# A trunk of matmuls whose 512-column streams are turned round

## The chip, the core and the metric

The kernel runs on one core of one Trainium2 chip. A core has a matmul engine (TensorE; PE in the profile, its weight loads PEld), three engines for elementwise work (VectorE or DVE, ScalarE or ACT, GpSimd or POOL), and a queue that issues DMAs (SyncE or SP). Matmuls read SBUF and write PSUM, which has banks of 512 float32 columns on 128 partitions. The metric is the device time of one execution in microseconds (us), given as the median of the runs.

## The reference

Two groups of 512 tokens (a prompt and a sample), 1024 wide, pass through the same two layers: differential attention with 8 heads, then a bidirectional retention with 8 heads. Both layers project, mix, normalise by head, gate and project back.

```python
def trunk(x, ...):
    for i in range(DEPTH):                        # DEPTH = 2
        h = rms_norm(x, norm_g[i], NORM_EPS)
        if i % N_MIXERS == 0:
            x = x + diff_attention(h, da_w_in[j], ...)
        else:
            x = x + bidir_retention(h, ret_w_in[j], ...)
    return rms_norm(x, final_norm_g, NORM_EPS)

def diff_attention(h, ...):
    q, k, v, gate = jnp.split(h @ w_in, ...)      # w_in: 1024 x 8192
    s = jnp.einsum('bqhd,bkhd->bhqk', rotary_half(q), rotary_half(k))
    p = softmax(s);  a = p[:, :, 0] - lam * p[:, :, 1]
    o = jnp.einsum('bhqk,bkhe->bqhe', a, v)
    return (rms_norm(o, subln_g, SUBLN_EPS) * silu(gate)) @ w_out   # w_out: 2048 x 1024

def bidir_retention(h, ...):
    q, k, v, gate = jnp.split(h @ w_in, ...)      # w_in: 1024 x 6144
    o = retention_direction(q, k, v, ...) + flip(retention_direction(flip(q), flip(k), flip(v), ...))
    return (rms_norm(o, subln_g, SUBLN_EPS) * silu(gate)) @ w_out
```

## The kernel before

Each float32 operand is split into two parts of a rounded float32 type (`hi_of`, L400, on ScalarE, and `lo_of`, L403, on VectorE), and each product is three matmuls, hi by hi, hi by lo and lo by hi (`PASSES`), added up in one PSUM bank.

**Projections.** The normalised activations of both token groups stand transposed in SBUF as the operands of a seven-product scheme (`Bop`, products P1 to P7). A `Unit` covers 256 columns of an input weight; of its two kinds, "pair" (queries, keys, gates) has weights stationary and streams 512 tokens, and "wide" (values) has activations stationary and streams 256 weight columns. `product` issues them: `pair` at L599, 12 matmuls of 512 columns for a product (4 slices of the contraction by 3 passes), `wide` at L609, 48 of 256 columns. Banks come from the rings `pj` (3), `sc` (2), `o` (2) and `tp` (1).

**Attention.** For each head, group and tile of 128 queries: `scores` (L1116) makes two score banks with 3 matmuls of 512 columns each, `row_max` (L1124) and `exps` (L1134) the softmax, `combine` the difference, `transp` (L1161) four transposes, and for every second tile `av` (L1181) 24 matmuls of 256 columns.

**Output projections.** `out_step` (L891) makes one block of 128 tokens by 512 columns of one head's contribution with 6 matmuls, and VectorE (L896) adds it to the residual. The last block of the second layer is done in two halves of 256 columns.

**Retention.** Its products (L1315, L1339, L1359, L1367) stream 256 columns.

Eight matmuls of 512 columns at L1010, on plain float32 zeros, run ahead of all work while the inputs arrive.

A planner (`Plan`) takes all operations with assumed costs, places them on the five engines in a simulated schedule, and writes out that order; what a matmul costs in it is a constant in the program (0.7 us for the three matmuls of `scores`, 2.79 for the twelve of `pair`, 1.39 for the six of `out_step`).

Of the kernel before, what the change touches and what calls it, by code (L numbers as in the profile page):

```python
# [15 lines left out]
P = 128  # L16
# [237 lines left out]
def trunk_kernel(  # L254
# [7 lines left out]
    nc = tc.nc  # L262
# [90 lines left out]
    def bank(tag, name=None):  # L353
        return Buf(plan, tag, BUFS[tag], lambda i: view(pj if tag == "pj" else sc, tag, i, S, [P, S]))
# [19 lines left out]
    def axpy(n, fn, r, w):  # L374

        plan.op("DVE", 0.13 + 0.00104 * n, fn, r, w)
# [13 lines left out]
    def pe(cost, fn, r, w, wait=0.0):  # L390
        plan.op("PE", cost, fn, r, w, wait=wait)
# [126 lines left out]
    class Unit:  # L518
# [67 lines left out]
        def product(self, op):  # L586
            which = BANK_OF[op]
            n_banks = 2 if self.wide else 1
            opens = op in OPENS
            if opens:  # L590
                self.banks[which] = [bank(self.tags[which], which) for _ in range(n_banks)]
            a, b = self.ops.pop(op), B_OF[op]
            bt = [Bop[b, k] for k in range(4)]
            reads = [q[1] for q in a] + bt

            def pair(ps, ks=range(4)):
                for k in ks:
                    for i, (u, v) in enumerate(PASSES):
                        nc.tensor.matmul(  # L599
                            ps.t, a[u][0]()[:, k, :], bt[k][:, v, :], start=(opens and k == 0 and i == 0),  # L600
                            stop=(k == 3 and i == 2), skip_group_check=True)

            def wide(ps, t):
                if self.led and op == "P1" and t == 0:
                    for j in range(NT):
                        nc.tensor.transpose(ps[:, j * P:(j + 1) * P], ident.t, ident.t)
                for k in range(4):
                    for i, (u, v) in enumerate(PASSES):
                        nc.tensor.matmul(  # L609
                            ps[:, (t % 2) * 256:(t % 2) * 256 + 256], bt[k][:, v, t * P:(t + 1) * P],  # L610
                            a[u][0]()[:, k, :], start=(opens and t % 2 == 0 and k == 0 and i == 0),
                            stop=(k == 3 and i == 2), skip_group_check=True)

            if not self.wide:
                ps = self.banks[which][0]
                if op == "P1" and self in first_units[:2]:
                    for k in range(4):
                        pe(0.7, lambda k=k: pair(ps, (k,)), reads[:2] + [bt[k]], [(ps, k)])
                else:
                    pe(2.79, lambda: pair(ps), reads, [ps])  # L620
                return
            for t in range(NT):
                ps = self.banks[which][t // 2]
                led = self.led and op == "P1" and t == 0
                pe(1.87 if led else 1.43, lambda ps=ps, t=t: wide(ps, t), reads + [ident] * led, [ps])
# [236 lines left out]
    def out_weights(w, h, i):  # L862
        r = raw_t([P, 2, S])
        src = w[h * 256:(h + 1) * 256, i * S:(i + 1) * S].rearrange("(e p) c -> p e c", p=P)
        dma(lambda: r.t, lambda: src, [], [r], 512)
        hi, lo = ws_t([P, 2, S]), ws_t([P, 2, S])
        hi_of(1024, lambda: hi.t, lambda: r.t, [r], [hi])
        lo_of(1024, lambda: lo.t, lambda: r.t, lambda: hi.t, [r, hi], [lo])
        wsn[h, i] = (hi, lo)

    def out_step(w, h, g, t, i, o, rr, last, parts=1):


        owed[h, g] -= 1
        if (h, i) not in wsn:
            out_weights(w, h, i)
        banks = [bank("pj") for _ in range(parts)]
        u = wsn[h, i]
        x = xN[g, t]
        n = S // parts  # L880
        for p in range(parts):
            here = slice(p * n, (p + 1) * n)
            part = (x, i) if parts == 1 else (x, (i, p))

            ps = banks[p]

            def fn(here=here, ps=ps):
                m = 0
                for e in range(2):
                    for a, b in PASSES:  # L890
                        nc.tensor.matmul(ps[:, here], o[a][:, e, t * P:(t + 1) * P], u[b][:, e, here],  # L891
                                         start=(m == 0), stop=(m == 5))
                        m += 1
            pe(1.39 / parts, fn, [(o[0], t // 2), (o[1], t // 2), *u], [ps])
            half = x[:, i * S + p * n:i * S + (p + 1) * n]
            axpy(n, lambda half=half, here=here, ps=ps: nc.vector.scalar_tensor_tensor(  # L896
                half, ps[:, here], rr[:, t % 2:t % 2 + 1], half, op0=ALU.mult, op1=ALU.add),
                [ps, part, rr], [part])
            if h == NH - 1:
                last(g, t, i, half, n, part, i == 1 and p == parts - 1)  # L900
# [206 lines left out]
    def scores(i):  # L1107
        h, g, t = tiles[i]
        st[i]['s'] = []
        for j in range(2):  # L1110
            s = bank("sc")
            q, k = qk[h, g, j, 0], qk[h, g, j, 1]

            def fn(s=s, q=q, k=k):
                for n, (a, b) in enumerate(PASSES):
                    nc.tensor.matmul(s.t, q[:, a, t * P:(t + 1) * P], k[:, b, :], start=(n == 0), stop=(n == 2))  # L1116
            pe(0.7, fn, [q, k], [s])
            st[i]['s'].append(s)

# [333 lines left out]
    for i in range(N2 + 1):  # L1453
        if i < N2:
            b, c = chunks[i]
# [78 lines left out]
```

## Time and profile before

| | |
|---|---|
| median of 3 runs | 1808.89 us (1808.3 to 1814.46) |
| span of the profiled execution | 1807.0 us |
| TensorE busy | 1794.9 us, 99% of the span |
| weight loads (PEld) | 1558.1 us, 86% |
| VectorE busy | 1477.1 us, 82% |
| ScalarE busy | 895.1 us, 50% |
| GpSimd busy | 169.5 us, 9% |
| DMA queue with the most traffic | 326.71 MB, 54.1% of 16 engines |

The span runs from the first to the last instruction of the profiled execution; that execution has no time of its own beside the span, and the median of the timed runs lies 1.9 us above it. A matmul's record in the profile is longer than the distance to the next matmul's start, because matmuls overlap in the engine and their ends are modelled; lengths of back-to-back pieces give the distance.

### The profile page before, as it was taken

The page shows a single profiled execution, that of the slowest core. Times are in us where ns is not written, and L with a number is a line of the kernel's source. Part 1 is how long each engine was busy: PE and PEld are TensorE (multiplying, and loading weights), DVE is VectorE, ACT ScalarE, POOL GpSimd, SP SyncE. Part 2 cuts the span into 40 slices and gives each one's busy share as a digit, 9 for nine tenths or more (in the row PEclk, how much of TensorE's full clock was granted, in tenths as well). Part 3 has the DMA queues.
Part 4 walks back from the last instruction along what each step waited for, and adds up shares of the span by engine and source line. Part 5 has one row for each costly group of instructions (what it writes and reads, how often), then busy time and mean ns, then how long its engine had stood idle before and what let it go on. Part 6 is the DMA issues. An engine that isn't in the chain of part 4 may idle for free.

```text
span 1807.0 us, 27780 instructions
## 1 busy us (share of the span) xinstructions
PE 1794.9 (99%) x10299; PEld 1558.1 (86%) x10299; DVE 1477.1 (82%) x2319; ACT 895.1 (50%) x1856; POOL 169.5 (9%) x323
## 2 busy tenths in 40 slices
PE   9999999999999999999999999999999999999998
PEld 6789889898988888888888888898989898888887
DVE  7958787778699888888888897787887967888887
ACT  7753444433434565554555866444434355444346
POOL 1000000000000022222322300000000000111113
PEclk9999999999999999999999999999999999999999
DMA  6444455555545685444554524464657559765662
GB/s 217 134 126 137 161 140 178 184 168 155 174 126 175 201 334 198 178 156 159 190 204 140 190 73 146 140 210 146 205 156 228 151 170 396 272 238 182 225 218 94
DMA packets 162767, 328.81 MB, mean 182 GB/s; under 512 B 12724, under 2 KB 76872, under 8 KB 162632
## 3 DMA queue, kind: packets, MB, share of 16 engines
q1 hardware_dynamic: 162304, 326.71, 54.1%
q8 instruction: 81, 1.33, 0.3%
q14 instruction: 54, 0.44, 0.1%
q10 hardware_dynamic: 328, 0.34, 0.1%
HBM read 209.55 MB, written 117.44 MB: 181 GB/s over the span
## 4 chain that ended last, share of the span: by engine, by line
PE 93%; DVE 2%; DMA 2%; ACT 2%; issue 1%; POOL 0%; SPq 0%; POOLq 0%; DVEq 0%; ACTq 0%
PE pj L599 20%; PE pj L891 19%; PE sc L599 10%; PE pj L609 10%; PE o L599 8%; PE o L1181 5%; PE sc L1116 5%; PE sc L609 5%; PE o L609 2%; PE o L1359 2%; PE tp L1161 2%; PE sc L1315 1%; PE o L1367 1%; PE tp L1339 1%; DMA raw<-in_ret_w_out_dram 1%
## 5 line engine op out<-in xcount | busy, mean ns | idle before, releaser
L891 PE MATMUL pj<-ws,arena 128*128 128x512 f32 x1542 | 391.2, 397 | 0.0
L891 PEld LDWEIGHTS pj<-ws,arena 128*128 128x128 f32 x1542 | 277.7, 188 | 52.7
L599 PE MATMUL pj<-b,ws 128*128 128x512 f32 x1080 | 265.0, 392 | 0.0
L599 PEld LDWEIGHTS pj<-b,ws 128*128 128x128 f32 x1080 | 201.4, 188 | 43.0
L403 DVE TENSOR_TENSOR ws<-st,ws 128x512 fp32r<-128x512 f32 (+1 forms) x192 | 147.9, 774 | 74.8 <-ACT ws L400 56.7
L896 DVE SCALAR_TENSOR_TENSOR b<-pj,crr,b 128x512 f32<-128x512 f32 (+1 forms) x257 | 189.9, 744 | 21.4 <-PE pj L891 21.0
L403 DVE TENSOR_TENSOR ws<-raw,ws 128x512 fp32r<-128x512 f32 (+1 forms) x164 | 141.5, 868 | 71.3 <-ACT ws L400 61.0
L400 ACT CAST ws<-st 128x512 fp32r<-128x512 f32 (+1 forms) x192 | 132.4, 693 | 121.4 <-PE pj L599 36.4
L599 PE MATMUL sc<-arena,ws 128*128 128x512 f32 x768 | 186.8, 392 | 0.0
L599 PE MATMUL o<-arena,ws 128*128 128x512 f32 x744 | 180.0, 393 | 1.1 <-ACT m L385 0.6
L599 PEld LDWEIGHTS sc<-arena,ws 128*128 128x128 f32 x768 | 144.0, 188 | 31.3
L400 ACT CAST ws<-raw 128x512 fp32r<-128x512 f32 (+1 forms) x164 | 125.7, 772 | 87.0 <-PE o L599 45.0
L599 PEld LDWEIGHTS o<-arena,ws 128*128 128x128 f32 x744 | 138.4, 188 | 31.7 <-DVE arena L463 1.4
L599 PE MATMUL pj<-arena,ws 128*128 128x512 f32 x648 | 160.3, 392 | 0.4 <-DVE arena L463 0.4
L599 PEld LDWEIGHTS pj<-arena,ws 128*128 128x128 f32 x648 | 120.8, 188 | 26.7 <-DVE arena L463 0.7
L1134 ACT ACTIVATE b<-sc,nm 128x512 f32<-128x512 f32 x128 | 88.0, 689 | 66.9 <-DVE nm L1124 66.5
L636 ACT COPY c<-pj 128x512 f32<-128x512 f32 x104 | 60.9, 586 | 119.7 <-PE pj L599 66.4
L609 PE MATMUL pj<-ws,b 128*128 128x256 f32 x960 | 116.8, 276 | 0.0
L609 PEld LDWEIGHTS pj<-ws,b 128*128 128x128 f32 x960 | 113.2, 188 | 0.7
L1116 PE MATMUL sc<-arena 128*128 128x512 f32 x384 | 101.2, 395 | 0.3 <-ACT b L1134 0.3
L1181 PEld LDWEIGHTS o<-arena 128*128 128x128 f32 x768 | 93.1, 188 | 2.7
L1181 PE MATMUL o<-arena 128*128 128x256 f32 x768 | 93.7, 278 | 0.0
(207 smaller groups left out, 2855.9 us busy)
## 6 DMA issues: line engine op xcount, KB each, us to landing
qk<-os SPq DMA_DIRECT2D x192, 256.0 KB, 3.6
arena<-qk SPq DMA_DIRECT2D x96, 512.0 KB, 5.8
raw<-in_da_w_in_dram SPq DMA_DIRECT2D x64, 512.0 KB, 5.1
v<-os SPq DMA_DIRECT2D x64, 512.0 KB, 4.3
arena<-v SPq DMA_DIRECT2D x64, 512.0 KB, 4.1
raw<-in_ret_w_in_dram SPq DMA_DIRECT2D x48, 512.0 KB, 4.8
os<-g SPq DMA_DIRECT2D x32, 512.0 KB, 7.4
g<-e SPq DMA_DIRECT2D x48, 256.0 KB, 4.6
```

Of the source, the lines that this page charges most:

```text
L400: act(n, lambda: nc.scalar.copy(dst(), src()), r, w)
L403: dve(n, lambda: nc.vector.tensor_tensor(dst(), src(), hi().bitcast(F32), op=ALU.subtract), r, w)
L599: nc.tensor.matmul(ps.t, a[u][0]()[:, k, :], bt[k][:, v, :], start=(opens and k == 0 and i == 0), stop=(k == 3 and i == 2), skip_group_che ...
L609: nc.tensor.matmul(ps[:, (t % 2) * 256:(t % 2) * 256 + 256], bt[k][:, v, t * P:(t + 1) * P], a[u][0]()[:, k, :], start=(opens and t % 2 == ...
L636: act(S, lambda c=c, ps=ps: nc.scalar.copy(c.t, ps.t), [ps], [c])
L891: nc.tensor.matmul(ps[:, here], o[a][:, e, t * P:(t + 1) * P], u[b][:, e, here], start=(m == 0), stop=(m == 5))
L896: axpy(n, lambda half=half, here=here, ps=ps: nc.vector.scalar_tensor_tensor(half, ps[:, here], rr[:, t % 2:t % 2 + 1], half, op0=ALU.mult ...
L1116: nc.tensor.matmul(s.t, q[:, a, t * P:(t + 1) * P], k[:, b, :], start=(n == 0), stop=(n == 2))
L1134: act(840, lambda j=j, s=s, m=m: nc.scalar.activation(p[:, j, :], s.t, AF.Exp, bias=m.t, accum_out=sm[:, 2 * j + n:2 * j + n + 1]), [s, m] ...
L1161: nc.tensor.transpose(tp[:, j * P:(j + 1) * P], p[:, 0, j * P:(j + 1) * P], ident.t)
L1181: nc.tensor.matmul(o[:, e * 256:(e + 1) * 256], v[b][:, j, e * P:(e + 1) * P], aT[a][:, j, :], start=(n == 0), stop=(n % 12 == 11), skip_g ...
L1359: nc.tensor.matmul(o[:, e * 256:(e + 1) * 256], v_[v][:, 2 * c + j, e * P:(e + 1) * P], a_[:, u, j * 256:(j + 1) * 256], start=(e == 0 and ...
```

## The change

In three places a matmul's moving operand and its PSUM output are indexed from the last column to the first, with a step of -1. Every column's sum lands where it did before, and within a bank all matmuls of a sum go in the same direction. The stationary operand is indexed as before.

```diff
@@ pair, in Unit.product @@
                         nc.tensor.matmul(
-                            ps.t, a[u][0]()[:, k, :], bt[k][:, v, :], start=(opens and k == 0 and i == 0),
+                            ps[:, ::-1], a[u][0]()[:, k, :], bt[k][:, v, ::-1], start=(opens and k == 0 and i == 0),
                             stop=(k == 3 and i == 2), skip_group_check=True)
@@ out_step @@
-                        nc.tensor.matmul(ps[:, here], o[a][:, e, t * P:(t + 1) * P], u[b][:, e, here],
+                        nc.tensor.matmul(ps[:, here][:, ::-1], o[a][:, e, t * P:(t + 1) * P], u[b][:, e, here][:, ::-1],
                                          start=(m == 0), stop=(m == 5))
@@ scores @@
-                    nc.tensor.matmul(s.t, q[:, a, t * P:(t + 1) * P], k[:, b, :], start=(n == 0), stop=(n == 2))
+                    nc.tensor.matmul(s[:, ::-1], q[:, a, t * P:(t + 1) * P], k[:, b, ::-1],
+                                     start=(n == 0), stop=(n == 2))
```

The last block of the second layer's output projection, in two halves of 256 columns, is indexed by the second of these places too.

## The prediction

> **What bounds the kernel now.** I read the page first: busy times, then the granted clock, then the chain of waits.
>
> ```profile
> span 1807.0 us, 27780 instructions
> PE 1794.9 (99%) x10299; PEld 1558.1 (86%) x10299; DVE 1477.1 (82%) x2319; ACT 895.1 (50%) x1856; POOL 169.5 (9%) x323
> PEclk9999999999999999999999999999999999999999
> PE 93%; DVE 2%; DMA 2%; ACT 2%; issue 1%; POOL 0%; SPq 0%; POOLq 0%; DVEq 0%; ACTq 0%
> ```
>
> TensorE has work in flight for 1794.9 of 1807.0 us, so it idles for only 12.1 us; it holds 93% of the chain that ended last, and its clock is granted at 90% or more in every slice. The next engine, DVE, is 330 us short of the span. The profiled execution spans 1807.0 us; the three timed runs have a median of 1808.89, so I add 1.9 us for what lies around the span. Then I asked what TensorE waited for (the view of waits, TensorE alone: us in total, times, longest).
>
> ```profile
> PE sc L1010 <- DVE minus L411: 1.4, 1, 1.4
> PE tp L1028 <- DVE arena L463: 1.0, 2, 0.7
> PE o L1028 <- DVE b L387: 0.6, 1, 0.6
> PE o L599 <- ACT m L385: 0.6, 1, 0.6
> ```
>
> These are the four longest lines; all waits together are under 5 us. There is next to no slack in which a longer matmul could hide and no stall that a shorter one would expose early: what one matmul gains or loses, the span gains or loses. So the question is the pace of one 512-column matmul, and the number of them. The instruction groups of TensorE, shapes kept apart (busy us, mean ns of one record):
>
> ```profile
> L891 PE MATMUL pj<-ws,arena 128*128 128x512 f32 x1530 | 389.8, 398 | 0.0
> L599 PE MATMUL pj<-b,ws 128*128 128x512 f32 x1080 | 265.0, 392 | 0.0
> L599 PE MATMUL sc<-arena,ws 128*128 128x512 f32 x768 | 186.8, 392 | 0.0
> L599 PE MATMUL o<-arena,ws 128*128 128x512 f32 x744 | 180.0, 393 | 1.1 <-ACT m L385 0.6 <-DVE arena L463 0.3
> L599 PE MATMUL pj<-arena,ws 128*128 128x512 f32 x648 | 160.3, 392 | 0.4 <-DVE arena L463 0.4
> L599 PE MATMUL sc<-b,ws 128*128 128x512 f32 x120 | 29.1, 391 | 0.0
> L1116 PE MATMUL sc<-arena 128*128 128x512 f32 x384 | 101.2, 395 | 0.3 <-ACT b L1134 0.3
> L609 PE MATMUL pj<-ws,b 128*128 128x256 f32 x960 | 116.8, 276 | 0.0
> L1161 PE MATMUL tp<-ident,b 128*128 128x128 f32 x256 | 38.4, 272 | 0.0
> ```
>
> L599 has 1080 + 768 + 744 + 648 + 120 = 3360 matmuls of 512 columns, L891 1530, L1116 384: 5274 that the change turns round. A record is longer than the pace, since matmuls overlap; the pace comes from the pieces of the chain (start us, length us, what), where nothing lies between instructions:
>
> ```profile
> 75.27 8.24 PE pj L599 x36
> 163.58 5.47 PE o L609 x48
> 705.89 1.39 PE pj L891 x6
> 707.28 2.83 PE o L1181 x24
> 710.11 1.40 PE sc L1116 x6
> 711.51 0.44 PE tp L1161 x4
> 713.35 1.38 PE sc L1116 x6
> 719.53 2.74 PE o L1181 x24
> ```
>
> Paces: L599 8.24/36 = 228.9 ns; L891 1.39/6 = 231.7; L1116 1.39/6 (mean of two pieces) = 231.7; 256 columns at L609 5.47/48 = 114.0; 128 columns at L1161 0.44/4 = 110. A record is thus its pace plus a tail that doesn't depend on the width: 392 - 228.9 = 163 at 512 columns, 276 - 114 = 162 at 256, 272 - 110 = 162 at 128. The 5274 take 3360 x 0.2289 + 1914 x 0.2317 = 769 + 443 = 1213 us, two thirds of the span.
>
> **The change, part by part.** No instruction is added, removed or moved: built from both kernels, the order on all five engines is the same, DMA issues included, and so is each count. What changes in a matmul is two patterns: the moving operand's (start at the last column, step -1 for 1) and the bank's. The weights' pattern stays. The eight warm-up matmuls, the 256-column ones (L609, L1181, L1315 and the rest) and the transposes stay as they are; only the split last block of L891, 12 matmuls of 256 columns, turns too, worth 12 x 0.1 = 1 us at half rate and left out of the sum.
>
> The semaphore waits change in 24 places, all on DVE. Five subtractions that write a weight split lose a wait for TensorE; DVE isn't the bound, so that is worth nothing. Nineteen of the row maxima over the scores gain a wait for ACT. What it protects is a column of the four-deep ring that the exponential two tiles earlier read; the scores' own matmul has already waited for a later exponential to free its bank, so I cost this at nothing. If that cover were gone, DVE would stand for one exponential each time:
>
> ```profile
> L1134 ACT ACTIVATE b<-sc,nm x128: 672/690/704, 628.1 to 1004.4; 128x512 f32<-128x512 f32 x128
> L1010 PE MATMUL sc<-e x16: 592/592/1220, 1.4 to 10.9; 128*128 128x512 f32 x16
> 1.44 10.09 PE L1010 MATMUL sc<-e 128*128 128x512 f32 x16 [1.44 <-DVE minus L411]
> ```
>
> 19 x 0.69 = 13 us of DVE, behind which are queued the combinations of the probabilities and the evacuations of the output banks; TensorE runs other blocks meanwhile, so under 13 us at the worst.
>
> What is left is the price of a descending column stream. No row shows one: every matmul of this trace reads and writes ascending, contiguous columns. The nearest rows give the bounds. The trace has two column rates at a granted clock of 90% or more. The fast one is 512 columns in 229 ns and 256 in 114: 2.2 columns per ns. The slow one is the last two rows above: L1010 streams the same 512 columns, and its record is 592 at the minimum and the median, so its pace is 592 - 163 = 429 ns, 1.2 columns per ns; the transposes of L1161, in the middle of the run, have 128 columns in 110 ns, 1.2 too. Those rows read plain float32 where the fast ones read the rounded kind, so the slow rate has its own reason there; what it shows is the step in which this engine falls back: to half. The fast rate takes two columns where the slow one takes one. [...]
>
> Bounds of the unknown price, per matmul: from below, the best column rate that any row shows, 2 x 114.0 = 228 ns, no loss and a gain of 1 to 4 ns; from above, L1010's first rows: if nine of its sixteen run at 429 (the median equals the minimum), the other seven take (10.09 - 0.16 - 9 x 0.429)/7 = 867 ns each, a quarter of the fast rate. Between these I take 429, the row of the same width, at the median of that group; and as the upper end of this case twice the best pace, 456 ns, where the small excess of the fast rate is doubled as well.
>
> The Trainium skill, page "SBUF — State Buffer", section "Door 1: The DMA port swizzle", speaks to both sides: reads within one 16-byte line run at full bandwidth from two hits in the line on, while a PSUM line holds two float32 values and any non-contiguous PSUM pattern slows matmuls significantly. Its first half would make the descending read free and the time that of before; its second half speaks against this change if a step of -1 counts as non-contiguous, and gives no figure. No row here shows either.
>
> The sum: L599 3360 x (429 - 228.9) = 672 us; L891 1530 x (429 - 231.7) = 302; L1116 384 x (429 - 231.7) = 76; together 1050 us. Nothing is taken off for waits that vanish (under 5 us). 1807 + 1050 + 1.9 = **2859 us**. With 456 ns for 429, 5274 x 0.027 = 142 us more: 3001. If all 12.1 us of TensorE's idle time were used up on the way, it would be 2847. So the case's own range is 2845 to 3000. DVE, ACT and DMA do the same work in a longer span and are never late.
>
> **The rivals.**
>
> *Direction is free.* The stream pairs columns by line, not by order; all four floats of a line are visited one after another either way. For it: each tile's last column ends where an ascending stream ends, so pairs fall into the same lines. Against it: nothing but the absence of a row. Time: 1809, no change.
>
> *Faster: the order relieves the weight loads.* The paces aren't uniform at one width: L1181 has pieces of 2.83 and of 2.74 us for the same 24 matmuls, L891 runs 2.8 ns slower than L599. TensorE loads weights for 86% of the span, out of the same memory as it streams from, and the weight read keeps its order while the stream turns: overlaps in address fall elsewhere. If all matmuls reached 228 ns: 3360 x 0.9 + 1914 x 3.7 = 10 us, giving 1799; it decides when the 512-column pace falls under 228 ns. Against it: L599, two thirds of these matmuls, stands already within 1 ns of that.
>
> *A little slower: more such conflicts.* If all 5274 take on the ratio of those two pieces, 2.83/2.74 = 1.033: 1213 x 0.033 = 40 us, giving 1849. For and against as above, with the sign turned.
>
> *Far slower.* Each column a read of its own at the pace of the warm-up's start: 5274 x (867 - 230) = 3360 us, giving 5169. For it: only that group's first rows. Against it: no row after 10 us shows it.
>
> *The change doesn't do what it says.* Both patterns turn in the built instructions, so this has no chance of its own.
>
> **How the numbers follow.** Half rate 0.52, since it needs only one of two sides to fail and the trace shows that very rate at this width; free 0.20; faster 0.14; a little slower 0.09; far slower 0.05. I call 0.5% (9 us) the bound of what a measurement tells here. Slower is 0.52 + 0.09 + 0.05 = 0.66, same 0.20, faster 0.14. The likeliest is the half rate, 2859 us. For 8 in 10 the range must reach down to the free case and the 10 us gain; a deeper gain and the far-slower case are left out: 1795 to 3000. The likeliest alone has 2845 to 3000.
>
> **What would show it.** In the profile of the changed kernel the groups of L599, L891 and L1116 should have means near 592 ns for 392 to 398, chain pieces of 36 of L599 15.4 us for 8.24, while L609 and L1181 stay at 276 and 278 ns. DVE should keep its 1477 us and fall from 82% to about 52% of the span. I am wrong if those groups keep 392 ns; and right for a wrong reason if the pace stays and waits grow, or if the granted clock leaves 9.

## The result: 1.1% slower, and the profile after

The changed kernel takes 1829.01 us (median of 4 runs, 1828.85 to 1829.38) beside 1808.71 us before (a fourth run joins the three of the table above); the ratio is 1.0106, with a 95% interval of 1.0091 to 1.012. Its profiled execution spans 1827.0 us for 1807.0. The page of the profile after, its parts on busy time, granted clock and chain:

```profile
span 1827.0 us, 27794 instructions
PE 1815.9 (99%) x10299; PEld 1559.7 (85%) x10299; DVE 1480.4 (81%) x2319; ACT 894.9 (49%) x1856; POOL 169.8 (9%) x323
PEclk9999999999999999999999999999999999999999
PE 94%; DVE 3%; DMA 1%; ACT 1%; issue 0%; POOL 0%; SPq 0%; POOLq 0%; DVEq 0%
```

TensorE's busy time grew by 21.0 us and the span by 20.0; its idle time stays nearly where it was (11.1 us for 12.1), which is the 1 us between the two; the other engines do the same work, and the mean granted clock is as before (0.999 of full speed in both). All of the loss is in matmuls. The groups of TensorE after, shapes kept apart (busy us, mean ns of one record):

```profile
L891 PE MATMUL pj<-ws,arena 128*128 128x512 f32 x1530 | 394.4, 402 | 0.0
L599 PE MATMUL pj<-b,ws 128*128 128x512 f32 x1080 | 269.7, 397 | 0.0
L1116 PE MATMUL sc<-arena 128*128 128x512 f32 x384 | 102.7, 399 | 0.3 <-ACT b L1135 0.3
L609 PE MATMUL pj<-ws,b 128*128 128x256 f32 x960 | 116.6, 276 | 0.0
```

The records of the turned matmuls are 4 to 5 ns longer (402 for 398, 397 for 392, 399 for 395), not 200. The 256-column group of L609, which wasn't touched, keeps its 276. The chain's pieces give the pace (start us, length us, what):

```profile
75.31 8.40 PE pj L599 x36
156.95 5.47 PE pj L609 x48
```

8.40/36 = 233.3 ns for 228.9 before. At 4.4 ns, the 3360 matmuls of L599 lose 14.9 us; L891's busy time grew by 394.4 - 389.8 = 4.6 us and L1116's by 102.7 - 101.2 = 1.5. That is 21.0 us, but it counts some overlap of neighbouring groups twice: start to start, the turned matmuls take 20 of the 21.0 us by which TensorE's busy time grew. The rest, 1 us net, comes from 256-column matmuls that nobody touched. Two groups of the retention got longer, here the larger one, before and after (line 1360 after the change is line 1359 before):

```profile
L1359 PE MATMUL o<-arena 128*128 128x256 f32 x384 | 48.9, 276 | 0.0
L1360 PE MATMUL o<-arena 128*128 128x256 f32 x384 | 50.3, 279 | 0.0
```

L1367 went from 27.0 to 27.8 us in the same way, while L1181 fell from 93.7 to 92.9.

### The profile page after: what moved, and what is told of

The parts are those of the page before. It is cut to its first block, busy times and chain, and to the rows that moved or that the text cites. A ratio compares the mean times of both kernels' runs of the same rounds, so it can differ in the third digit from the quotient of the medians.

```text
span 1827.0 us, 27794 instructions
## 1 busy us (share of the span) xinstructions
PE 1815.9 (99%) x10299; PEld 1559.7 (85%) x10299; DVE 1480.4 (81%) x2319; ACT 894.9 (49%) x1856; POOL 169.8 (9%) x323
## 4 chain that ended last, share of the span: by engine, by line
PE 94%; DVE 3%; DMA 1%; ACT 1%; issue 0%; POOL 0%; SPq 0%; POOLq 0%; DVEq 0%
PE pj L599 21%; PE pj L891 19%; PE sc L599 11%; PE pj L609 10%; PE o L599 8%; PE sc L1116 5%; PE o L1182 5%; PE sc L609 5%; PE o L609 2%; PE o L1360 2%; PE tp L1162 2%; PE o L1368 1%; PE sc L1316 1%; PE tp L1340 1%; DMA raw<-in_ret_w_out_dram 1%; DVE ws L403 1%
## 5 line engine op out<-in xcount | busy, mean ns | idle before, releaser
L891 PE MATMUL pj<-ws,arena 128*128 128x512 f32 x1542 | 395.8, 401 | 0.0
L891 PEld LDWEIGHTS pj<-ws,arena 128*128 128x128 f32 x1542 | 278.1, 188 | 55.9
L599 PE MATMUL pj<-b,ws 128*128 128x512 f32 x1080 | 269.7, 397 | 0.0
L599 PEld LDWEIGHTS pj<-b,ws 128*128 128x128 f32 x1080 | 201.6, 188 | 47.3
L599 PE MATMUL sc<-arena,ws 128*128 128x512 f32 x768 | 190.2, 397 | 0.0
L599 PE MATMUL o<-arena,ws 128*128 128x512 f32 x744 | 183.2, 398 | 1.1 <-ACT m L385 0.6
L599 PEld LDWEIGHTS sc<-arena,ws 128*128 128x128 f32 x768 | 144.1, 188 | 34.6
L599 PEld LDWEIGHTS o<-arena,ws 128*128 128x128 f32 x744 | 138.5, 188 | 34.6 <-DVE arena L463 1.4
L599 PE MATMUL pj<-arena,ws 128*128 128x512 f32 x648 | 163.2, 397 | 0.4 <-DVE arena L463 0.3
L599 PEld LDWEIGHTS pj<-arena,ws 128*128 128x128 f32 x648 | 121.0, 188 | 29.3 <-DVE arena L463 0.7
L609 PE MATMUL pj<-ws,b 128*128 128x256 f32 x960 | 116.6, 276 | 0.0
L609 PEld LDWEIGHTS pj<-ws,b 128*128 128x128 f32 x960 | 113.0, 188 | 0.8
L1116 PE MATMUL sc<-arena 128*128 128x512 f32 x384 | 102.7, 399 | 0.3 <-ACT b L1135 0.3
L1182 PE MATMUL o<-arena 128*128 128x256 f32 x768 | 92.9, 277 | 0.0
```

The lines of the kernel that those rows point to most:

```text
L599: nc.tensor.matmul(ps[:, ::-1], a[u][0]()[:, k, :], bt[k][:, v, ::-1], start=(opens and k == 0 and i == 0), stop=(k == 3 and i == 2), skip ...
L609: nc.tensor.matmul(ps[:, (t % 2) * 256:(t % 2) * 256 + 256], bt[k][:, v, t * P:(t + 1) * P], a[u][0]()[:, k, :], start=(opens and t % 2 == ...
L891: nc.tensor.matmul(ps[:, here][:, ::-1], o[a][:, e, t * P:(t + 1) * P], u[b][:, e, here][:, ::-1], start=(m == 0), stop=(m == 5))
L1116: nc.tensor.matmul(s[:, ::-1], q[:, a, t * P:(t + 1) * P], k[:, b, ::-1], start=(n == 0), stop=(n == 2))
L1182: nc.tensor.matmul(o[:, e * 256:(e + 1) * 256], v[b][:, j, e * P:(e + 1) * P], aT[a][:, j, :], start=(n == 0), stop=(n % 12 == 11), skip_g ...
```

## The experiments

All turn or vary the 512-column matmuls of L599, L891 and L1116 in the kernel before, unless said otherwise. The diffs show L599; the other two places have the same edit. Each ratio is to the kernel before as it was timed beside that run (medians from 1808.5 to 1809.61 us), so times of different experiments with the same ratio can differ a little.

### Which side costs: read and write apart

```diff
-  ps.t,        a[u][0]()[:, k, :], bt[k][:, v, :]
+  ps.t,        a[u][0]()[:, k, :], bt[k][:, v, :][:, ::-1]     # e1_read
+  ps.t[:, ::-1], a[u][0]()[:, k, :], bt[k][:, v, :]            # e2_write
```

> Only the moving operand of the 512-column matmuls is read from its last column; the bank is written ascending, so each block's columns come out in reverse. Theory R (the descending read costs the 4 ns): the pace of L599 is 233.3 ns, as with both turned, time 1829 us. Theory W (the descending write costs it): pace 229 to 230, time 1809. Theory B (each side costs a part): about 1819. A read that must be descending together with the write, since the two cancel otherwise, would show as a time above 1829.

> Only the bank is written from its last column; the moving operand is read ascending, so each block's columns come out in reverse. Theory R: 1809 us, L599 at 229 to 230 ns in its cycle of 226, 229 and 232. Theory W: 1829 us, 233.3 ns throughout. Theory B: about 1819.

Measured: the read alone 1829.13 us, ratio 1.0114 (1.0097 to 1.0131); the write alone 1808.63 us, ratio 1.0001 (0.9991 to 1.0011). The read carries all of it, the write nothing. The chain's pieces, first of the read alone, then of the write alone:

```profile
75.58 8.40 PE pj L599 x36
```

```profile
75.25 8.24 PE pj L599 x36
```

With the read turned, L599 has the 233.3 ns of the changed kernel; with the write turned, the 228.9 of before. The changed semaphore waits drop out as a cause as well: the profile of the write alone has the changed kernel's 27794 instructions, 14 more than before (nineteen gained waits less five lost), and loses nothing; the read alone has the 27780 of before and loses all.

### Is it a price of each matmul?

> Both sides turned at L599 alone (3360 of 5274 matmuls). If the cost is one of each matmul, L599's starts are 234.6 ns apart on average for 230.4 before: 3360 x 4.1 ns = 13.8 us of the 20, time 1822 to 1823, and L891 and L1116 keep the pace of before. If the cost comes from how a long run of turned matmuls leaves the engine (a state carried over), it is not in proportion: L891 and L1116 slow down too and the time is near 1829, or L599 itself recovers and it is near 1809.

Only the first hunk of the change was kept. Measured: 1822.02 us, ratio 1.0074 (1.0059 to 1.0089), as expected for a price of each matmul. Its groups:

```profile
L891 PE MATMUL pj<-ws,arena 128*128 128x512 f32 x1530 | 389.8, 398 | 0.0
L599 PE MATMUL pj<-b,ws 128*128 128x512 f32 x1080 | 269.8, 398 | 0.0
L1116 PE MATMUL sc<-arena 128*128 128x512 f32 x384 | 101.3, 395 | 0.3 <-ACT b L1134 0.3
```

L599 stands as in the changed kernel, L891 and L1116 as before.

### Does it hold at 256 columns?

```diff
-  ps[:, (t % 2) * 256:(t % 2) * 256 + 256], bt[k][:, v, t * P:(t + 1) * P], a[u][0]()[:, k, :]
+  ps[:, (t % 2) * 256:(t % 2) * 256 + 256][:, ::-1], bt[k][:, v, t * P:(t + 1) * P], a[u][0]()[:, k, ::-1]
   # and likewise in av, score2, state2, near and other; on top of the change
```

> As the changed kernel, and the 4416 matmuls of 256 columns (L609, L1181 and the retention's) turned too, both sides. If a descending stream always falls into the slower of the two paces that the width has (113.3 or 117.6 ns at 256 columns, both seen before and after), then 4416 x about 3.4 ns = 15 us more: 1844 us. If at 256 columns the weight load of the next matmul sets the pace, nothing: 1829 us.

Measured: 1848.11 us, ratio to before 1.0219 (1.0203 to 1.0234): 19.1 us on top of the change, for the 15 expected. The chain and a group of this run:

```profile
165.71 5.76 PE o L609 x48
```

```profile
L609 PE MATMUL pj<-ws,b 128*128 128x256 f32 x960 | 122.0, 282 | 0.0
```

5.76/48 = 120.0 ns for the 114.0 of before: 6 ns a matmul. That is more than the 117.6 ns which I had taken for the slower of two paces; at 256 columns a turned stream can hold a steady pace slower than either. But it isn't everywhere at that pace. Another piece of the same run:

```profile
197.90 5.07 PE pj L609 x43
```

This is 5.07/43 = 117.9 ns, about the slower of the two known paces, and over all 4416 matmuls the 19.1 us come to 4.3 ns each. The direction of the expectation held, its size was short. Read and write were turned together here; at this width no run separates them.

### At which scale the direction matters

The stream was read in blocks of n columns, the blocks from the last to the first and ascending inside, or the other way round; the write stayed ascending.

```diff
-  bt[k][:, v, :]
+  bt[k][:, v, :].rearrange("p (a b) -> p a b", b=4)[:, ::-1, ::1]    # r_lines; b=32, 64, 128, 256: r_blk32, r_blk64, r_blk128, r_halves
+  bt[k][:, v, :].rearrange("p (a b) -> p a b", b=4)[:, ::1, ::-1]    # r_inside
```

> Read side only: groups of 4 columns (16 bytes) from the last to the first, ascending inside a group; the bank is written ascending, so columns come out permuted. Theory S (the stream's walk through memory against the weight load's matters, at a coarse scale): 233.3 ns at L599, 1829 us. Theory L (the order of neighbours inside 16 bytes matters, pairs being fetched together): 229 to 230 ns, 1809 us. Theory D (any walk but the plain one costs, through the pattern's dimensions): slower than 1829.

> Read side only: groups of 4 columns ascending, the four inside a group from the last to the first. Theory S: the walk is ascending at every scale over 16 bytes, so 229 to 230 ns and 1809 us. Theory L: 233.3 ns and 1829 us. Theory D: slower than 1829, as the groups from the last to the first.

> Read side only: blocks of 32 columns (128 bytes) from the last to the first, ascending inside. The excess of the fast pace over 2 columns per tick is 1 tick per 32 columns in the traces. Theory S: 233.3 ns if the scale that matters is over 128 bytes, near 229 if it is below. Theory L: 229. Theory D: as the 4-column groups.

> Read side only: the second 256 columns first, then the first 256, both ascending. Changes only where a stream starts and ends. If the cost of the turned read is one of the seam between two matmuls (each starts far from where the last one ended), this shows it: 233 ns, 1829 us. Theories S and L: 229 to 230 ns, 1809 us.

> Read side only, real weights: blocks of 128 columns (512 bytes) from the last to the first, ascending inside. Blocks of 32 gave 1828, of 256 1808. If what counts is the walk within the stretch in which a weight load runs beside the stream (128 weights at half the stream's rate, so 256 columns), blocks of 128 cost about half, 1818 us; if it is the walk within some hundred bytes, nothing, 1809.

> Read side only: blocks of 64 columns (256 bytes) from the last to the first, ascending inside. Blocks of 32 columns cost 19 us, blocks of 128 nothing. If the read is served in pieces of up to 128 bytes and each jump back costs, 64 should cost part of it, about 1815 to 1820; if in pieces of 256 bytes, nothing, 1809.

| read order | ascending run | us | ratio to before (95%) |
|---|---|---|---|
| r_inside: 4 turned inside, groups ascending | - | 1808.72 | 1.0003 (0.9994 to 1.0013) |
| e1_read: all turned | 1 column | 1829.13 | 1.0114 (1.0097 to 1.0131) |
| r_lines | 4 columns, 16 bytes | 1829.26 | 1.0110 (1.0092 to 1.0128) |
| r_blk32 | 32 columns, 128 bytes | 1827.76 | 1.0102 (1.0086 to 1.0118) |
| r_blk64 | 64 columns, 256 bytes | 1808.69 | 1.0003 (0.9993 to 1.0013) |
| r_blk128 | 128 columns, 512 bytes | 1808.66 | 0.9996 (0.9987 to 1.0006) |
| r_halves | 256 columns, 1024 bytes | 1808.33 | 1.0000 (0.9990 to 1.0009) |

The order of neighbours inside 16 bytes is worth nothing, and neither is where a stream starts, ends or jumps, so long as it runs forward for 256 bytes at a time. With the blocks in descending order and shorter than that, the loss is there nearly whole: a step between runs of 128 and of 256 bytes, not a slope. The chain's pieces for runs of 128 and of 256 bytes:

```profile
75.20 8.40 PE pj L599 x36
```

```profile
74.66 8.24 PE pj L599 x36
```

The mean pace for runs of 128 bytes is that of the turned stream, but its pattern isn't: single starts there lie 236 and 230 to 231 ns apart in turn, where the turned stream has 233 to 234 throughout. Theory L is out (neighbours), so is the seam, so is Theory D (a pattern of three dimensions costs nothing in itself: r_inside, r_blk64). The walk matters, at a scale over 128 and up to 256 bytes. For r_blk64 I had named two outcomes, a part of the loss for pieces of up to 128 bytes and nothing for pieces of 256; it was nothing, which fits pieces of 256 bytes but doesn't show them.

### Is it the weight load beside the stream?

My rival in the prediction had the two reads colliding. Two pairs of runs test that. In the first, all weights of the 512-column matmuls are one column read 128 times; in the second, two of three weight loads at L599 have half as many columns, and their records last 134 ns for 188.

```diff
-  ps.t, a[u][0]()[:, k, :], ...
+  ps.t, a[u][0]()[:, k, :][:, 0:1].broadcast_to([P, P]), ...         # w0_asc; with the read turned: w0_desc
+  ps[0:P >> (i > 0)], a[u][0]()[:, k, 0:P >> (i > 0)], ...           # h_asc, L599 alone; with the read turned: h_desc
```

> As before, but the weights of the 512-column matmuls are one column of 128 read over and over (step 0), so that a weight load touches one place in memory and walks nowhere; the products are other numbers. Theory S1 (the stream's walk falls against the weight load's walk): the pace leaves the cycle of 226, 229, 232 ns and goes to one value, 226 to 227 ns, the time to about 1792 us (5274 x 3 ns less). Theory S2 (the walk of the stream alone matters): 229 to 230 ns as before, 1809 us.

> The same weights of one column, with the moving operand read from its last column (the write stays ascending). Theory S1: the same pace as the ascending read with these weights, within 1 ns, so the same time as that run. Theory S2: 233.3 ns, 20 us above that run.

> At L599 the second and third pass load only the first 64 weight columns and add into the first 64 partitions, so two of three weight loads there are half as long and the lower half of the output lacks these passes; the stream is ascending. Theory P (the weight load beside the stream stalls it): the pace falls from 229.2 towards 227 ns for those, the time by about 2240 x 2 ns = 5 us, to about 1804. Theory A (the stream alone has these paces): 229 to 230 ns and 1809, or any move has another cause.

> The same half-size loads at L599, the moving operand there read from its last column. Theory P: the 8 ticks (6.7 ns) that a turned matmul pays over 226.7 halve beside a half load, so two of three matmuls go from 233.3 to 230 ns: about 1822 less 7 us, 1815. Theory A: 233.3 ns throughout L599, and 13 to 14 us above the ascending run with the same loads.

Measured: one-column weights 1819.61 us ascending (ratio 1.0057, 1.0042 to 1.0072) and 1839.67 turned (1.0169, 1.0152 to 1.0186); half loads 1809.02 ascending (0.9999, 0.9989 to 1.0008) and 1823.38 turned (1.0082, 1.0067 to 1.0097). The difference of the half-load pair, 14.4 us, is what turning L599 costs with full loads (13.5). The chain's pieces of the two turned runs, weights of one column first:

```profile
75.31 8.40 PE pj L599 x36
165.21 5.65 PE o L609 x48
```

```profile
75.34 8.40 PE pj L599 x36
```

A turned stream stands at 233.3 ns in both: beside weights that walk nowhere, and beside shorter loads. So neither the walk nor the length of the weight load makes that pace; Theory P and Theory S1 are out for the turned stream, and S2 and A, by which the stream alone has the pace, came out as expected. No run took the weight load away altogether. That the difference of the first pair is 20 us again is a coincidence of two parts. Its ascending run is itself disturbed, and the turned one is disturbed elsewhere; the chain's pieces of the ascending run:

```profile
75.13 8.34 PE pj L599 x36
156.18 5.47 PE pj L609 x48
```

Ascending with one-column weights, L599 has 8.34/36 = 231.7 ns, so what the weight load reads does touch an ascending stream's pace: with the walk taken away the pace got slower, where Theory S1 had expected it to fall. To the turned 233.3 only 1.6 ns are left. And in the turned run L609, whose matmuls and weights nobody touched, goes from 114.0 to 5.65/48 = 117.7 ns, which makes up most of the rest: a group of untouched matmuls can change its pace with what its neighbours do, as L1359 did in the changed kernel. Why, these runs don't show.

### What sets the pace of an ascending stream

In the single records of L599 before, starts lie 226, 229 and 232 ns apart in turn, as the three passes do. Three runs took away, at L599 alone, what differs between the passes.

```diff
-  ps.t, a[u][0]()[:, k, :], bt[k][:, v, :]
+  ps.t, a[0][0]()[:, k, :], bt[k][:, v, :]      # c_w: same weights in all passes
+  ps.t, a[u][0]()[:, k, :], bt[k][:, 0, :]      # c_m: same stream in all passes
+  ps.t, a[0][0]()[:, 0, :], bt[k][:, 0, :]      # c_wm: both, and the same weights for all k
```

> Ascending everywhere; at L599 all three passes take the upper part of the weights, so the third pass has the weights of the first two (its product is the wrong one). If the cycle follows the weights' place, the third value (232) goes or the cycle changes; if it follows the stream's place, it stays 226, 229, 232 and 1809 us.

> Ascending everywhere; at L599 all three passes stream the upper part of the operand, so the second streams what the first and third do. If the cycle follows the stream's place, it goes, to one value between 226 and 233; if it follows the weights', it stays, and 1809 us.

> Ascending everywhere; at L599 all twelve matmuls of a product take the same 128 weights and all three passes the upper part of the operand. If the cycle comes from where the two reads start, it goes: one value, 226 (3360 x 3 = 10 us less, 1799) or 233 (1822). If it still cycles in threes, it isn't the places, and comes from the engine's own rhythm.

Measured: 1809.16, 1809.54 and 1809.48 us, ratios 1.0000 (0.9990 to 1.0009), 1.0001 (0.9992 to 1.0011) and 0.9996 (0.9987 to 1.0005). The single records of L599 go on in the same cycle of 226, 229 and 232 ns in all three; a group of the third:

```profile
L599 PE MATMUL pj<-b,ws 128*128 128x512 f32 x1080 | 264.9, 392 | 0.0
```

That is before's 265.0 us and 392 ns. So which of the passes' weights or streams is read doesn't set the cycle. What does, these runs don't show; a rhythm of the engine itself, which the third expectation named, was only argued. No version with 226 ns throughout came out of this, and none here beats the kernel before.

## Why the prediction was wrong

**What bounds the kernel: right.** The forecast that each nanosecond of a matmul goes straight into the span held: 21.0 us more of TensorE's busy time, 20.0 us more span, no new wait of TensorE.

**Nothing is moved, and the changed waits are free: right.** DVE's busy time went from 1477.1 to 1480.4 us, the chain still lies on TensorE, the matmuls account for the whole loss, and e2_write, with as many instructions as the changed kernel, takes the time of before.

**The price of a descending stream: this step failed.** The prediction took 429 ns from L1010, "the row of the same width", on the ground that the half rate "needs only one of two sides to fail". Measured: 233.3 ns at L599. One side does have a price, the read, but it is 4.4 ns and not a fall to half (e1_read); the write has none (e2_write). The row of L1010 was of the same width but of another operand type, which the prediction itself named and then set aside. Nor is one record there one matmul of the program: the eight matmuls of L1010 stand as sixteen records. No turned matmul of the rounded type came near 429 ns in any run here. The sum was thus mis-sized in one term, 200 ns for about 4 on each of 5274 matmuls; 1829 lies in the range of 1795 to 3000 us only because that reached down to the free case, and outside the likeliest case's own 2845 to 3000. That the forecast "slower", with 0.66, came out is luck in the same way: 0.52 of it stood on the half rate.

Better rows were in the trace of before. The timeline of TensorE, before, in the retention stage (start us, length us):

```profile
1497.06 2.91 PE L599 MATMUL pj<-b,ws 128*128 128x512 f32 x12
1500.91 2.96 PE L599 MATMUL pj<-b,ws 128*128 128x512 f32 x12
```

Two blocks of the same twelve matmuls, ascending, with nothing waited for inside them: less the tail of 0.16 us, 2.75/12 = 229 and 2.80/12 = 233.3 ns. The second pace is that of a turned stream, and its single starts lie 232 to 234 ns apart throughout; so this pace is open to an ascending stream too, and a backward read isn't its only cause. It is the only one of L599's 280 blocks that has it throughout, and that turned streams would take just this pace is known only now. In hindsight, a forecast from these two rows, "all blocks take the slower pace that one already has", gives 5274 x 4.4 ns = 23 us, 1832 us.

**The rivals.** "A little slower", with 0.09, came nearest in kind: it said that the stream has paces a few per cent apart at one width and that turning it could bring the slower one. Its 1849 us misses by 20 us, as far as the free case on the other side. It took the ratio from L1181 (1.033) where L599's own was 233.3/228.9 = 1.019. Its mechanism, a collision with the weight load, isn't borne out: the turned pace stays with one-column weights and with shorter loads (w0_desc, h_desc). "Direction is free" failed for blocks under 256 bytes, though it was right for the order inside 16. In the Trainium skill, page "SBUF — State Buffer", section "Door 1: The DMA port swizzle", the rule of two hits in a 16-byte line agrees with r_inside, which costs nothing. It doesn't account for r_lines and e1_read: they too visit each line's four values one after another, and lose 1.1%. Its sentence that any non-contiguous PSUM pattern slows matmuls significantly doesn't reach to a step of -1: e2_write has a ratio of 1.0001.

What stays open is the cause under the 256 bytes. A read in pieces of that size would explain the step between r_blk32 and r_blk64, but was only argued. A price for each piece would also give a 256-column matmul half of the 4.4 ns, and it lost 4.3 ns on average and 6.0 in the slowest pieces; that speaks against it, or for a second part.

## What to carry to other kernels

When an operation's new form shows in no row, look first for a spread within the rows of its old form: here two paces of the same instruction at the same width were a far better guide to a change of access order than a slow row of another type, though at 256 columns the turned stream went beyond both, to 120.0 ns. In this kernel a 512-column stream could be reordered at no cost as long as it ran forward for 256 bytes at a time, or only inside each 16 bytes, and its bank could be written in either direction; read wholly backward or in descending blocks of up to 128 bytes it lost up to 2% of a matmul. With 256 columns, read and write turned together, the loss was 4% on average. Separate the read and the write first: one pair of runs halved the question.

## What the runs showed of the hardware

- A stream of 512 columns of the rounded float32 type, read backward, runs at 233.3 ns a matmul for 228.9 (8.40 and 8.24 us for 36). One of 256 columns, read and written backward, runs at up to 120.0 for 114.0 (5.76 and 5.47 us for 48).
- With blocks in descending order, the step lies between forward runs of 128 bytes (1827.76 us) and of 256 bytes (1808.69 us). The order inside 16 bytes doesn't matter (1808.72 us).
- Turning the write of the 512-column matmuls alone changes nothing: 1808.63 us for 1808.5.
- The pace of back-to-back matmuls has several settled values at one width, and a group that isn't changed can move from one to another with changes elsewhere: L609 from 114.0 to 117.7 ns when the weights at L599, L891 and L1116 became one column and their streams were turned. An ascending block of L599 in the kernel before has the turned stream's 233.3 ns.
